# Delta-rule scan on four quarters of the array, differential attention's values product in query halves, and the order planned anew

## The chip, the cores and the metric

The program runs on one core of a Trainium2 chip. The metric is the device time of one execution in microseconds (us); lower is better. Engines: PE multiplies matrices, DVE, ACT and POOL work element by element, SP issues most DMAs; each runs its own instructions in the order in which they stand, and waits where an operand is not there yet.

## What is computed

One layer over 256 tokens of width 1024. The branches share one projection; each has heads of width 64, four of them, and its own gate.

```python
h = rmsnorm(x, pre_norm_g[l])
proj = jnp.einsum('btd,dc->btc', h, w_in[l])          # (256 x 1024) @ (1024 x 4104)
p_gdn, p_hgrn, p_moba, p_diff = jnp.split(proj, splits, axis=-1)
y = jnp.concatenate([gdn_branch(p_gdn, ...), hgrn2_branch(p_hgrn, ...),
                     moba_branch(p_moba, ...), diff_branch(p_diff, ...)], axis=-1)
y = jnp.einsum('btc,cd->btd', y, w_out[l])
x = x + rmsnorm(y, post_norm_g[l])
```

The two places that change are the scan of the gated delta rule (chunks of 64 tokens, so four steps) and the last product of differential attention:

```python
def step(S, inp):
    q_c, k_c, u_c, w_c, a_c, d_c = inp
    v_new = u_c - w_c @ S
    o = q_c @ S + a_c @ v_new
    S = S * d_c[..., None, None] + jnp.einsum('bhcd,bhce->bhde', k_c, v_new)
    return S, o
...
outs.append(jnp.einsum('bhqk,bhkd->bhqd', a1 - lam * a2, v[:, :, :e]))
```

## The kernel before

**How work is recorded and ordered.** The program first records every operation in a `Core` object, and only then issues them, all from one line (L392 in the profile; table loads of ACT from L390). Between the two stands `plan()`, a list scheduler: each operation has a rank, which is its longest path to the end plus a fixed lead for the part of the program to which it belongs (`LEAD`: g the delta rule, h HGRN2, m and M the two parts of MoBA, d and D those of differential attention, o the output projection, x the rest); each engine takes the ready operation of highest rank, except that a change of ACT's function table is put off by up to `HOLD` of rank and a change of PE's tiling mode by up to `STAY`. The sequence that results is fixed in the program.

**Projections.** Weights arrive by DMA as `raw` blocks, which ACT rounds to `whi` and DVE turns into a remainder `wlo`; the activations stand likewise as `hT_hi` and `hT_lo`. Each tile of a projection takes three products (hi by hi, lo by hi, hi by lo) into a bank `pj`. These are most of PE's work, and the filling between all other steps.

**Delta rule.** Before the scan, an inverse of each 64x64 chunk matrix is made: 15 steps of substitution inside 16x16 blocks on DVE (`g_nb`, `g_y`), a transposition by DVE into `g_xa`, products `gA<-g_xa,g_ee` and `gB<-g_ya,g_za`, and the same once more with 32x32 tiles. The scan (lines 804 to 840) then has four steps n. Two heads share the 128 partitions, head hh on partitions 64hh to 64hh+63; two such pairs hp make four products per operation. In step n > 0: `kb` by the state `st` into bank gB, DVE subtracts (`g_r`), and `qd` by `st` into bank gA (`po`, which collects o of all steps). Then the inverse by `g_r` into gB, which ACT copies to `g_vn`; for n < 3 `kd` by `g_vn` into gB and DVE's new state `g_s`; and `aq` by `g_vn` into gA. In the trace `kb` and `qd` both read as g_eb, `kd` as g_kdec and `aq` as g_ee. All of these products use a 64x64 quarter of the array, always the same two: rows 0 to 63 with columns 0 to 63, and rows 64 to 127 with columns 64 to 127. Each is float32 and leaves two records in the trace, so four products are x8.

**Differential attention.** `attend` multiplies transposed probabilities (`d_pt`, 128 keys by 128 queries) by values (`v_diff`, 128 keys by 64), 12 products of full height and width into one bank wB, which leave 24 records. Its logits (`wB<-d_st`) read operands that POOL's queue assembles by 24 DMA copies from `d_ks` and `qk4k`.

**The end.** Output projection (`pj<-whi,y_gdn` and on, into pj and gA), a norm on ACT and DVE, four output DMAs.

Of the kernel before, what the change touches and what calls it, by code (L numbers as in the profile page):

```python
# [29 lines left out]
D = 1024  # L30
# [61 lines left out]


class Op:
    __slots__ = ("eng", "fn", "args", "kw", "cost", "need", "preds", "succs", "rank", "left", "at", "order", "boost", "groups", "work", "part", "lat", "mode")


class Core:
# [2 lines left out]

    SETS = {AF.Exp: 6, AF.Ln: 6, AF.Silu: 18}
    OUT = ("out", "accum_out", "dst")
    HOLD = 34479
    SWITCH, KEEP, STAY = 95, 1e9, 8733
    LEAD = {'h': 7522, 'g': 6523, 'o': -111940, 'M': 5144, 'x': 39478, 'm': 28417, 'd': 3696, 'D': 2624}
    WINDOW = 4096 / 1.2
    LAT = {"PE": 200, "DVE": 170, "ACT": 170, "POOL": 170, "SP": 2600}

    def __init__(self, ctx, tc):  # L110
        self.tc, self.nc = tc, tc.nc
        nc = tc.nc
        self.sb = ctx.enter_context(tc.tile_pool(name="sb", bufs=1))
        self.ps = ctx.enter_context(tc.tile_pool(name="ps", bufs=1, space=bass.MemoryType.PSUM))
        ctx.enter_context(tc.manual_schedule())
        self.engines = {"PE": nc.tensor, "DVE": nc.vector, "ACT": nc.scalar, "POOL": nc.gpsimd, "SP": nc.sync}
        self.ops = []
        self.boost, self.part = 0.0, "x"
        self.phys, self.turn, self.masks = {}, {}, {}
        self.sbuf, self.psum = {}, {}  # L120

# [50 lines left out]
    def record(self, eng, fn, cost, writes, reads, args, kw, need=None):  # L172
        op = Op()
        op.eng, op.fn, op.args, op.kw, op.cost, op.need = eng, fn, args, kw, cost, need
        op.preds, op.succs, op.boost, op.groups, op.work = set(), [], self.boost, (0, 1, 2, 3), 0.0
        op.part, op.lat, op.mode = self.part, self.LAT[eng], (128, 128)
        me = len(self.ops)
        for w, aps in ((False, reads), (True, writes)):
            for ap in aps:
                name = ap.tensor.name  # L180
                if name in self.psum:

                    b = self.psum[name]
                    if b[0] != eng:
                        b[0], b[1], b[2] = eng, b[2], []
                    if me not in b[2]:
                        op.preds.update(b[1])
                        if eng == "PE":

                            start = kw.get("start", True)  # L190
                            op.preds.update(i for i in b[2] if start or self.ops[i].kw.get("start", True))
                        b[2].append(me)
                    continue
                q, m = self.region(ap)
                log = self.sbuf.setdefault(name, [])
                keep = []
                for e in log:
                    i, wi, qi, mi = e
                    hit = (w or wi) and q & qi and m & mi and i != me
                    if hit:  # L200
                        op.preds.add(i)
                    if not (hit and w and qi & ~q == 0 and mi & ~m == 0):
                        keep.append(e)
                keep.append((me, w, q, m))
                self.sbuf[name] = keep
        self.ops.append(op)
# [17 lines left out]
    def mm(self, out, lhsT, rhs, start=True, stop=True, **kw):  # L224
        n, m = self.size(rhs), lhsT.shape[1]
        full = 1.667 if rhs.dtype == F else .417
        cost = max(n * full, m * full) + 2 if rhs.dtype == F else max(n * .446, 107) + 4.5
        self.record("PE", "matmul", cost, [out], [lhsT, rhs], (out,),
                    dict(lhsT=lhsT, rhs=rhs, start=start, stop=stop, **kw))
        p, m = self.rows(out)  # L230
        o = self.ops[-1]
        if 2 < m < 128:
            o.groups = tuple(range(p // 32, (p + m + 31) // 32))
        k = self.rows(rhs)[1]
        o.mode = (32 if k <= 32 else 64 if k <= 64 else 128 if k > 96 else 96, 32 if m <= 32 else 64 if m <= 64 else 128)
        o.work = n * full * k / 128

    def tr(self, out, in_, ident):
# [56 lines left out]
    def plan(self, noise=None):  # L295

        import heapq
        ops = self.ops
# [9 lines left out]
        for i, o in enumerate(ops):  # L308
            o.rank += o.boost + (self.LEAD.get(o.part, 0.0) if o.boost < BOOST else 0.0)
            if noise is not None:  # L310
                o.rank += noise[i]
        ready = {e: [] for e in self.engines}
        free = dict(PE=1150.0, DVE=880.0, ACT=800.0, POOL=0.0, SP=800.0)
        events = [(0.0, 0, i) for i, o in enumerate(ops) if not o.left]
        due = {}
        heapq.heapify(events)
        order, cur = [], 6
        cols, mode, work = [0.0] * 4, (128, 128), {}
        while events:
            t = events[0][0]  # L320
            while events and events[0][0] <= t:
                _, kind, i = heapq.heappop(events)
                if kind == 0:
                    heapq.heappush(ready[ops[i].eng], (-ops[i].rank, i))
            for e, q in ready.items():
                if not q or free[e] > t:
                    continue
                i = heapq.heappop(q)[1]
# [29 lines left out]
                if e == "PE":  # L358

                    if o.mode != mode:  # L360
                        o.at = max(t, max(cols) + self.SWITCH)
                        mode = o.mode
                    else:
                        o.at = max([t] + [cols[g] for g in o.groups])
                    k = int((o.at + 630) / self.WINDOW)
                    slow = 1 if work.get(k - 1, 0.0) >= .41 * self.WINDOW else 2
                    work[k] = work.get(k, 0.0) + o.work
                    end = o.at + cost * slow
                    for g in o.groups:
                        cols[g] = end  # L370
                    free[e] = end if len(o.groups) == 4 else o.at + 7 * slow
                heapq.heappush(events, (free[e], 1, -1))
                for s in o.succs:
                    n = ops[s]
# [31 lines left out]
def _build(c, x, pxt, w_in, w_out, cst, prow, out, dbg):  # L406
# [231 lines left out]
    def gdn(pv, pab, sq):  # L638
# [168 lines left out]
        kd5 = kd.rearrange("p j q hp d -> p (j q) hp d")  # L807
        vb5 = vb.rearrange("p j q hp d -> p (j q) hp d")
        heads = [(hp, hh, slice(64 * hh, 64 * hh + 64)) for hp in range(2) for hh in range(2)]
        pair = lambda p: p[:, 0:128].rearrange("p (a b) -> p a b", a=2)  # L810
        for n in range(4):
            tok = slice(n * 64, (n + 1) * 64)
            rr = vb5[:, n]
            if n:
                pw = c.bank("gB")
                for hp, hh, r in heads:
                    mm(pw[r, hp * 64:(hp + 1) * 64], kb[r, hp, tok], st[r, hp, :])
                rr = c.tmp("g_r", [128, 2, 64])
                c.tt(rr, vb5[:, n], pair(pw), OP.subtract)
                for hp, hh, r in heads:  # L820
                    mm(po[r, (n * 2 + hp) * 64:(n * 2 + hp + 1) * 64], qd[r, hp, tok], st[r, hp, :],
                       start=False, stop=False, skip_group_check=True)
            pw = c.bank("gB")
            for hp, hh, r in heads:
                mm(pw[r, hp * 64:(hp + 1) * 64], ya4[r, hp, n, :], rr[r, hp, :])
            vn = c.tmp("g_vn", [128, 2, 64])
            act(vn, pair(pw), AF.Copy)
            if n < 3:
                pw = c.bank("gB")
                for hp, hh, r in heads:  # L830
                    mm(pw[r, hp * 64:(hp + 1) * 64], kd5[r, n, hp, :], vn[r, hp, :])
                if n == 0:
                    c.copy(st, pair(pw))
                else:
                    for hp in range(2):
                        c.stt(st[:, hp, :], st[:, hp, :], ed[:, hp, n:n + 1], pw[:, hp * 64:(hp + 1) * 64],
                              OP.mult, OP.add)
            for hp, hh, r in heads:
                mm(po[r, (n * 2 + hp) * 64:(n * 2 + hp + 1) * 64], aq[r, hp, n, :], vn[r, hp, :],
                   start=(n == 0 and hp == 0), skip_group_check=True)  # L840

        s8 = c.tile("g_s8", [128, 8])
        head_norm(s8, po.rearrange("p (a b) -> p a b", a=8), c.tmp("t2k", [128, 8, 64]))
# [3 lines left out]
        po5 = po.rearrange("p (j q hp d) -> p j q hp d", j=2, q=2, hp=2)  # L847
        for hh in range(2):
            for q in range(2):
                r = slice(64 * hh, 64 * hh + 64)  # L850
                c.tt(y[64 * q:64 * q + 64].rearrange("p j (hp hh d) -> p j hp hh d", hp=2, hh=2)[:, :, :, hh, :],
                     po5[r, :, q, :, :], bc(s84[r, :, q, :], 64), OP.mult)
        c.tt(y, y, gz["gdn"], OP.mult)
# [144 lines left out]
    def attend(pt, vm, bank):  # L998

        po = c.bank(bank)  # L1000
        for j in range(2):
            for h in range(4):
                hp, hh = h // 2, h % 2
                o = (j * 4 + h) * 64
                for b in range(j + 1):
                    i = hp if j == 0 else 2 + hp * 2 + b
                    mm(po[:, o:o + 64], pt[:, hh, i, :], vm[:, b, h * 64:(h + 1) * 64], start=(b == 0), stop=(b == j))
        return po.rearrange("p (a d) -> p a d", d=64)

    def attend_t(pt, vm, bank):  # L1010
# [249 lines left out]
```

## Time and profile before

| what | us |
|---|---|
| time, median of 3 runs (lowest, highest) | 168.05 (167.80, 168.16) |
| the profiled execution | 168.47 |
| its span, first to last instruction | 166.7 |
| PE busy | 157.4 (94%) |
| DVE busy | 133.0 (80%) |
| ACT busy | 108.3 (65%) |
| POOL busy | 18.8 (11%) |

The profiled execution lies 168.47 - 166.7 = 1.8 us over its span, and 0.42 us over the median. A record of PE runs from issue to a modelled end, and records overlap: x8 of mean 220 ns may fill 0.23 us. The step from start to start is therefore the cost of one, not its duration. The chain of waits gives such steps directly: each row there is the time that a piece adds to the chain.

### The profile page before, as it was taken

To read this page: it belongs to the slowest core of one execution; us is meant where nothing else is said; L and a number is where in the kernel's file an instruction comes from. 1 tells how busy PE (TensorE), PEld (TensorE's weight loads), DVE (VectorE), ACT (ScalarE), POOL (GpSimd) and SP (SyncE) were. 2 spreads that over 40 slices of the span, in tenths; PEclk is the share of its full clock that TensorE was granted. 3 is DMA by queue.
4 is the path that set the end of the run, shared out by engine and by line. 5 is a ranking of instruction groups with operands and counts; after the bars stand their busy time and mean duration, and the time that the engine had idled before them with its cause. 6 is when DMAs were issued, how large, how long until landed. Compare 5 with 4: busy or idle time off the path is not lost.

```text
span 166.7 us, 3622 instructions
## 1 busy us (share of the span) xinstructions
PE 157.4 (94%) x1351; PEld 138.1 (83%) x1351; DVE 133.0 (80%) x356; ACT 108.3 (65%) x214; POOL 18.8 (11%) x39
## 2 busy tenths in 40 slices
PE   7899999999999999997999999999999999999950
PEld 5699999999886989996899968877778798987850
DVE  0779589998999999996898598699699977428472
ACT  3678459999169986550059987999599353650450
POOL 8600000000001000077065200000000000000000
PEclk9999999999999999999999999999999999999998
DMA  5999998177870005936359886148603400000033
GB/s 165 317 413 412 361 397 322 29 241 225 275 261 0 0 4 168 309 91 128 127 153 243 179 264 240 34 145 286 236 0 129 126 0 4 0 0 0 0 126 126
DMA packets 14256, 27.24 MB, mean 163 GB/s; under 512 B 1440, under 2 KB 2720, under 8 KB 14240
## 3 DMA queue, kind: packets, MB, share of 16 engines
q1 hardware_dynamic: 12944, 25.31, 44.8%
q0 software_dynamic: 1152, 1.57, 4.8%
q8 instruction: 10, 0.16, 0.4%
q10 hardware_dynamic: 144, 0.15, 0.3%
q14 instruction: 6, 0.05, 0.1%
HBM read 24.14 MB, written 1.05 MB: 151 GB/s over the span
## 4 chain that ended last, share of the span: by engine, by line
PE 60%; DVE 23%; DMA 9%; issue 3%; ACT 2%; SPq 1%; DVEq 0%; ACTq 0%
PE pj L392 39%; DMA raw<-in_w_in_dram 9%; PE gA L392 7%; PE gB L392 6%; PE wB L392 4%; PE wA L392 4%; DVE g_nb L392 4%; DVE wlo L392 3%; DVE g_ee L392 2%; DVE y L392 1%; DVE g_kdec L392 1%; DVE g_y L392 1%; DVE prob L392 1%; ACT whi L392 1%; DVE g_vb L392 1%
## 5 line engine op out<-in xcount | busy, mean ns | idle before, releaser
L392 DVE TENSOR_TENSOR wlo<-raw,whi 128x1024 fp32r<-128x1024 f32 (+2 forms) x42 | 48.3, 1173 | 12.4 <-ACT whi L392 7.6
L392 ACT ACTIVATE whi<-raw 128x1024 fp32r<-128x1024 f32 (+2 forms) x41 | 41.0, 1023 | 6.8 <-DMA raw<-in_w_in_dram 3.6
L392 PE MATMUL pj<-hT_hi,whi 128*128 128x256 f32 x144 | 36.8, 289 | 0.7 <-ACT hT_hi L392 0.7
L392 PE MATMUL pj<-hT_lo,whi 128*128 128x256 f32 x144 | 36.5, 288 | 0.0
L392 PE MATMUL pj<-hT_hi,wlo 128*128 128x256 f32 x144 | 28.7, 284 | 0.0
L392 PEld LDWEIGHTS pj<-hT_hi,whi 128*128 128x128 f32 x144 | 26.6, 190 | 1.9 <-ACT hT_hi L392 1.4
L392 PEld LDWEIGHTS pj<-hT_lo,whi 128*128 128x128 f32 x144 | 26.3, 188 | 0.3 <-issue 0.2
L392 PE MATMUL pj<-whi,hT_lo 128*128 128x512 f32 (+2 forms) x80 | 26.3, 348 | 0.0
L392 PEld LDWEIGHTS pj<-hT_hi,wlo 128*128 128x128 f32 x144 | 22.0, 189 | 0.4 <-issue 0.2
L392 PE MATMUL pj<-whi,hT_hi 128*128 128x512 f32 (+2 forms) x64 | 21.2, 344 | 0.0
L392 PE MATMUL pj<-wlo,hT_hi 128*128 128x512 f32 (+2 forms) x64 | 19.9, 353 | 0.2 <-DVE wlo L392 0.2
L392 PEld LDWEIGHTS pj<-whi,hT_lo 128*128 128x128 f32 x80 | 15.0, 188 | 1.6
L390 ACT ACT_TABLE_LOAD x11 | 14.1, 1283 | 1.4 <-PEq L1250 1.2
L392 PEld LDWEIGHTS pj<-whi,hT_hi 128*128 128x128 f32 x64 | 12.0, 189 | 1.2
L392 PEld LDWEIGHTS pj<-wlo,hT_hi 128*128 128x128 f32 x64 | 11.1, 189 | 1.6 <-DVE wlo L392 0.4
L392 ACT ACTIVATE prob<-prob,mx 128x128 f32<-128x128 f32 (+1 forms) x24 | 10.6, 445 | 0.1
L392 DVE CUSTOM_DVE_ANT_0 prob<-wB,cs 128x128 f32<-128x128 f32 (+1 forms) x24 | 8.0, 354 | 1.7 <-PE wB L392 1.6
L392 PE MATMUL pj<-whi,d_st 128*128 128x512 f32 (+1 forms) x32 | 9.1, 371 | 0.0
L392 POOL MEMSET vexp<- 128x1024 f32 x3 | 2.8, 948 | 46.6 <-PE wB L392 46.6
L392 POOL DMA_DIRECT2D d_st<-d_ks x12 | 6.2, 514 | 16.8 <-ACT d_ks L392 16.8
L392 ACT ACTIVATE t2k<-pj 128x512 f32<-128x512 f32 (+1 forms) x4 | 2.2, 544 | 8.9 <-PE pj L392 8.9
L392 ACT ACTIVATE g_za<-gA 32x256 f32<-32x256 f32 x2 | 0.8, 376 | 9.9 <-PE gA L392 9.8
(271 smaller groups left out, 301.0 us busy)
## 6 DMA issues: line engine op xcount, KB each, us to landing
raw<-in_w_in_dram SPq DMA_DIRECT2D x26, 512.0 KB, 5.5
raw<-in_w_out_dram SPq DMA_DIRECT2D x8, 512.0 KB, 4.8
raw<-in_w_in_dram SPq DMA_DIRECT2D x4, 520.0 KB, 9.9
raw<-in_w_in_dram SPq DMA_DIRECT2D x4, 256.0 KB, 4.1
xs<-in_x_dram SPq DMA_DIRECT2D x2, 512.0 KB, 8.4
prob<-in_pxt_dram SPq DMA_DIRECT2D x3, 256.0 KB, 6.1
d_st<-d_ks POOLq DMA_DIRECT2D x12, 64.0 KB, 3.1
d_st<-qk4k POOLq DMA_DIRECT2D x12, 64.0 KB, 3.5
```

The source lines that it names most:

```text
L390: nc.scalar.add_instruction(mybir.InstLoadActFuncSet(name=nc.get_next_instruction_name(), act_func_set_id=cur, ins=[], outs=[]))
L392: getattr(self.engines[o.eng], o.fn)(*o.args, **o.kw)
```

## The change

**Scan.** `qd` by `st` and `aq` by `g_vn` (the side products) write `po` on the other half of the partitions (`other[hh]`), so they use the two quarters that were idle: rows 0 to 63 with columns 64 to 127, and the reverse. `both()` records them pair by pair behind the chain products `kb` by `st` and `kd` by `g_vn`, and gives the eight of a group one rank (`tie`), the highest among them. The last step's `aq` (n = 3) has no chain product beside it. The assembly of y reads `po` from the other half. No operation is added.

**attend.** Each 128x128x64 product becomes two of 64 queries, on the left and the right 64 columns of the array: 24 products for 12.

**Planner.** The model of PE holds 16 quarters' ends in place of four column groups, adds 20 ns to a product that does not fill the array, and has other numbers for `HOLD`, `STAY` and all of `LEAD`. The sequences of all engines are thus planned anew. PE's first 309 rows stay the same; behind them they differ everywhere.

```diff
-    HOLD = 34479
-    SWITCH, KEEP, STAY = 95, 1e9, 8733
-    LEAD = {'h': 7522, 'g': 6523, 'o': -111940, 'M': 5144, 'x': 39478, 'm': 28417, 'd': 3696, 'D': 2624}
+    HOLD = 10718
+    SWITCH, KEEP, STAY = 95, 1e9, 10757
+    LEAD = {'h': 2055, 'g': 7404, 'o': -103025, 'M': 12770, 'x': 27161, 'm': 33539, 'd': 8615, 'D': -9392}
...
+        a, b = (range(x // 32, (x + n) // 32) if n < 96 else range(4) for x, n in ((q, o.mode[0]), (p, o.mode[1])))
+        o.groups = tuple(4 * i + j for i in a for j in b)
+        if len(o.groups) < 16:
+            o.cost += 20
...
+        for tied in ties.values():
+            top = max(o.rank for o in tied)
+            for o in tied:
+                o.rank = top
...
+        other = [slice(64, 128), slice(0, 64)]
+        def both(name, chain, side):
+            c.tie = name
+            for hp in range(2):
+                for f in (chain, side):
+                    for a, hh, r in heads[2 * hp:2 * hp + 2]:
+                        f(a, hh, r)
+            c.tie = None
...
-                for hp, hh, r in heads:
-                    mm(pw[r, hp * 64:(hp + 1) * 64], kb[r, hp, tok], st[r, hp, :])
+                both(f"g{n}s", lambda hp, hh, r: mm(pw[r, hp * 64:(hp + 1) * 64], kb[r, hp, tok], st[r, hp, :]),
+                     lambda hp, hh, r: mm(po[other[hh], (n * 2 + hp) * 64:(n * 2 + hp + 1) * 64], qd[r, hp, tok],
+                                          st[r, hp, :], start=False, stop=False, skip_group_check=True))
                 rr = c.tmp("g_r", [128, 2, 64])
                 c.tt(rr, vb5[:, n], pair(pw), OP.subtract)
-                for hp, hh, r in heads:
-                    mm(po[r, (n * 2 + hp) * 64:(n * 2 + hp + 1) * 64], qd[r, hp, tok], st[r, hp, :],
-                       start=False, stop=False, skip_group_check=True)
...
+            pw = c.bank("gB") if n < 3 else None
+            both(f"g{n}v", lambda hp, hh, r: pw is None or mm(pw[r, hp * 64:(hp + 1) * 64], kd5[r, n, hp, :], vn[r, hp, :]),
+                 lambda hp, hh, r: mm(po[other[hh], (n * 2 + hp) * 64:(n * 2 + hp + 1) * 64], aq[r, hp, n, :],
+                                      vn[r, hp, :], start=(n == 0 and hp == 0), skip_group_check=True))
...
-                    mm(po[:, o:o + 64], pt[:, hh, i, :], vm[:, b, h * 64:(h + 1) * 64], start=(b == 0), stop=(b == j))
+                    for u in (slice(0, 64), slice(64, 128)):
+                        mm(po[u, o:o + 64], pt[:, hh, i, u], vm[:, b, h * 64:(h + 1) * 64], start=(b == 0), stop=(b == j))
```

**Where rows moved: PE in the scan, second step.** Before, from the inverse's product to the next projection tile:

```order
L392 MATMUL gB_118<-g_r_141,g_ya 64x64 x4
L392 MATMUL pj_94<-wlo_104,hT_hi 128x512
L392 MATMUL pj_94<-whi_103,hT_lo 128x512
L392 MATMUL gB_118<-g_vn_142,g_kdec 64x64 x4
L392 MATMUL gA_83<-g_vn_142,g_ee 64x64 x4
L392 MATMUL pj_94<-whi_103,hT_hi 128x512
```

Now:

```order
L401 MATMUL gB_118<-g_r_141,g_ya 64x64 x4
L401 MATMUL pj_94<-whi_103,hT_lo 128x512
L401 MATMUL wA_78<-ident,prob_69 128x128 x2
L401 MATMUL gB_118<-g_vn_142,g_kdec 64x64 x2
L401 MATMUL gA_83<-g_vn_142,g_ee 64x64 x2
L401 MATMUL gB_118<-g_vn_142,g_kdec 64x64 x2
L401 MATMUL gA_83<-g_vn_142,g_ee 64x64 x2
L401 MATMUL pj_94<-whi_103,hT_hi 128x512
```

Four chain products and four side products, which stood one behind the other, now alternate in twos. There are six such groups.

**PE at the values product of differential attention.** Before:

```order
L392 MATMUL gA_83<-ident,m_pt 128x128 x4
L392 MATMUL wB_150<-v_diff,d_pt 128x64 x4
L392 MATMUL pj_94<-whi_97,y_gdn 128x512
L392 MATMUL pj_95<-whi_97,y_gdn 128x512
L392 MATMUL pj_109<-whi_97,y_gdn 128x512
L392 MATMUL pj_94<-whi_100,y_gdn 128x512
L392 MATMUL pj_95<-whi_100,y_gdn 128x512
L392 MATMUL gB_118<-vexp_86,h_kd 64x256 x4
L392 MATMUL gA_83<-vexp_87,h_kd 64x192 x4
L392 MATMUL wB_150<-v_diff,d_pt 128x64 x7
L392 MATMUL gB_118<-m_pt,kf 128x128 x4
```

Now:

```order
L401 MATMUL gB_118<-vexp_86,h_kd 64x256 x4
L401 MATMUL gA_83<-vexp_87,h_kd 64x192 x4
L401 MATMUL wB_150<-v_diff,d_pt 64x64 x10
L401 MATMUL pj_110<-wlo_104,hT_hi 128x512
...
L401 MATMUL pj_109<-whi_97,y_gdn 128x512
L401 MATMUL wB_150<-v_diff,d_pt 64x64 x14
L401 MATMUL gB_118<-h_v,ath 128x64 x4
```

The product, before in runs of 1, 4 and 7, stands in runs of 10 and 14 halves; the first of them right behind HGRN2's 64-column products.

**DVE ahead of the inverse's first transposition.** Before, from the third substitution step from the end:

```order
L392 TENSOR_TENSOR g_nb_134<-g_nb_134,g_y_133 128x8x2
L392 TENSOR_TENSOR g_y_133<-g_y_133,g_nb_134 128x8x2
L392 TENSOR_TENSOR g_nb_135<-g_nb_135,g_y_133 128x8
L392 TENSOR_TENSOR g_y_133<-g_y_133,g_nb_135 128x8
L392 TENSOR_TENSOR g_ya<-g_y_133,cs 128x512
L392 STREAM_TRANSPOSE g_xa<-g_ya 128x512
```

Now:

```order
L401 TENSOR_TENSOR wlo_98<-raw_102,whi_97 128x2x512
L401 TENSOR_TENSOR wlo_101<-raw_105,whi_100 128x2x512
L401 TENSOR_TENSOR wlo_104<-raw_111,whi_103 128x2x512
L401 TENSOR_TENSOR wlo_107<-raw_112,whi_106 128x2x512
L401 TENSOR_TENSOR g_nb_135<-g_nb_135,g_y_133 128x8
L401 TENSOR_TENSOR qk4k<-qk4k 128x512
L401 TENSOR_TENSOR g_y_133<-g_y_133,g_nb_135 128x8
L401 TENSOR_TENSOR gz_moba<-pj_95,rrow 128x512
L401 TENSOR_TENSOR g_ya<-g_y_133,cs 128x512
L401 STREAM_TRANSPOSE g_xa<-g_ya 128x512
```

Four `wlo` splits and `gz_moba`, which stood behind `g_xa`, and the last split of `qk4k`, which stood seven substitution steps earlier, now stand close ahead of it. On PE, the products that read `g_xa` moved too: 437 projection products stand ahead of them before, 476 now.

## Rows read from the trace of the kernel before

**Rows 1.** The page: busy time of each engine, share of the span, instructions.

```profile
PE 157.4 (94%) x1351; PEld 138.1 (83%) x1351; DVE 133.0 (80%) x356; ACT 108.3 (65%) x214; POOL 18.8 (11%) x39
```

**Rows 2.** The page: the chain that ended last, shares by engine.

```profile
PE 60%; DVE 23%; DMA 9%; issue 3%; ACT 2%; SPq 1%; DVEq 0%; ACTq 0%
```

**Rows 3.** Windows: stretch, its length, busy time per engine; PE clock, DMA share, GB/s.

```profile
25.00:77.20 52.20, 50.84 (x426) 47.42 (x425) 50.45 (x171) 38.79 (x77) 6.08 (x12) 1.00 0.51 159
77.20:160.80 83.60, 83.54 (x759) 69.59 (x759) 64.13 (x150) 53.65 (x109) 6.71 (x14) 1.00 0.39 116
```

**Rows 4.** Chain of waits, scan's last steps: start, us added, engine, written bank, records.

```profile
112.35 0.38 PE gB L392 x8
112.73 0.23 PE gA L392 x8
112.96 1.14 PE pj L392 x4
...
117.06 0.40 PE gA L392 x8
```

**Rows 5.** Groups by shape on PE: the side products that read g_vn.

```profile
L392 PE MATMUL gA<-g_vn,g_ee 64*64 64x64 f32 x32 | 1.6, 221 | 0.0
```

**Rows 6.** Chain of waits, values product of differential attention.

```profile
128.38 0.84 PE wB L392 x8
...
132.12 1.71 PE wB L392 x14
```

**Rows 7.** Timeline of PE: the first of these products and what follows; start, us.

```profile
122.99 0.33 PE L392 MATMUL wB<-v_diff,d_pt 128*128 128x64 f32 x2
123.14 1.18 PE L392 MATMUL pj<-wlo,hT_hi 128*128 128x512 f32 x4
```

**Rows 8.** Chain of waits, MoBA's values product (wB) and HGRN2's state products (gB, gA).

```profile
110.85 1.50 PE wB L392 x16
...
137.87 0.41 PE gB L392 x19
...
138.45 0.27 PE gA L392 x15
138.71 0.43 PE pj L392
```

**Rows 9.** Timeline of PE: the shapes of those products.

```profile
110.78 1.57 PE L392 MATMUL wB<-m_pt,v_moba 128*64 128x256 f32 x16
...
138.07 0.25 PE L392 MATMUL gA<-sall,m_pt 64*32 64x64 f32 x3
138.11 0.23 PE L392 MATMUL gB<-sall,m_pt 64*32 64x64 f32 x3
```

**Rows 10.** Timeline of PE ahead of the inverse; in brackets idle time, and who ended it.

```profile
74.81 0.29 PE L392 MATMUL pj<-hT_lo,whi 128*128 128x256 f32 x1
74.93 0.28 PE L392 MATMUL pj<-hT_hi,whi 128*128 128x256 f32 x1
...
77.19 1.15 PE L392 MATMUL gA<-g_xa,g_ee 64*64 64x64 f32 x32 [1.03 <-DVE g_xa L392]
...
80.48 0.44 PE L392 MATMUL wB<-d_st 128*128 128x128 f32 x2
```

**Rows 11.** Timeline of DVE: a split, what follows it, and rows up to the transposition.

```profile
65.86 1.22 DVE L392 TENSOR_TENSOR wlo<-raw,whi 128x1024 fp32r<-128x1024 f32 x1
66.99 0.25 DVE L392 TENSOR_TENSOR g_y<-g_y,g_nb 128x88 f32<-128x88 f32 x1
...
73.20 0.69 DVE L392 TENSOR_TENSOR qk4k<-qk4k 128x512 fp32r<-128x512 f32 x1
...
75.70 0.69 DVE L392 TENSOR_TENSOR g_ya<-g_y,cs 128x512 f32<-128x512 f32 x1
76.43 0.71 DVE L392 STREAM_TRANSPOSE g_xa<-g_ya 128x512 f32<-128x512 f32 x1
...
88.53 0.69 DVE L392 TENSOR_TENSOR gz_moba<-pj,rrow 128x512 f32<-128x512 f32 x1
```

**Rows 12.** Timeline of POOL's queue, and the copies' time to landing.

```profile
74.66 0.50 POOL L392 DMA_DIRECT2D d_st<-d_ks  x1
...
DMA to landing us min/median/max: 1.8/3.3/5.8
```

**Rows 13.** Chain of waits: PE's last piece.

```profile
159.74 1.08 PE gA L392 x9
```

More of the change, by code (lines that the diff above doesn't have):

```diff
@@ L94 @@
 class Op:
-    __slots__ = ("eng", "fn", "args", "kw", "cost", "need", "preds", "succs", "rank", "left", "at", "order", "boost", "groups", "work", "part", "lat", "mode")
+    __slots__ = ("eng", "fn", "args", "kw", "cost", "need", "preds", "succs", "rank", "left", "at", "order", "boost", "groups", "work", "part", "lat", "mode", "tie")
 class Core:
@@ L117, in __init__ @@
         self.ops = []
-        self.boost, self.part = 0.0, "x"
+        self.boost, self.part, self.tie = 0.0, "x", None
         self.phys, self.turn, self.masks = {}, {}, {}
@@ L174, in record @@
         op.eng, op.fn, op.args, op.kw, op.cost, op.need = eng, fn, args, kw, cost, need
-        op.preds, op.succs, op.boost, op.groups, op.work = set(), [], self.boost, (0, 1, 2, 3), 0.0
-        op.part, op.lat, op.mode = self.part, self.LAT[eng], (128, 128)
+        op.preds, op.succs, op.boost, op.groups, op.work = set(), [], self.boost, range(16), 0.0
+        op.part, op.lat, op.mode, op.tie = self.part, self.LAT[eng], (128, 128), self.tie
         me = len(self.ops)
@@ L229, in mm @@
                     dict(lhsT=lhsT, rhs=rhs, start=start, stop=stop, **kw))
[L230 to L234, printed above, removed]
+        (p, m), (q, k), o = self.rows(out), self.rows(rhs), self.ops[-1]
         o.mode = (32 if k <= 32 else 64 if k <= 64 else 128 if k > 96 else 96, 32 if m <= 32 else 64 if m <= 64 else 128)
+        a, b = (range(x // 32, (x + n) // 32) if n < 96 else range(4) for x, n in ((q, o.mode[0]), (p, o.mode[1])))
+        o.groups = tuple(4 * i + j for i in a for j in b)
+        if len(o.groups) < 16:
+            o.cost += 20
         o.work = n * full * k / 128
@@ L311, in plan @@
                 o.rank += noise[i]
+        ties = {}
+        for o in ops:
+            if o.tie is not None:
+                ties.setdefault(o.tie, []).append(o)
+        for tied in ties.values():
+            top = max(o.rank for o in tied)
+            for o in tied:
+                o.rank = top
         ready = {e: [] for e in self.engines}
@@ L317, in plan @@
         order, cur = [], 6
-        cols, mode, work = [0.0] * 4, (128, 128), {}
+        cols, mode, work = [0.0] * 16, (128, 128), {}
         while events:
@@ L370, in plan @@
                         cols[g] = end
-                    free[e] = end if len(o.groups) == 4 else o.at + 7 * slow
+                    free[e] = end if len(o.groups) == 16 else o.at + 12 * slow
                 heapq.heappush(events, (free[e], 1, -1))
@@ L827, in gdn @@
             act(vn, pair(pw), AF.Copy)
+            pw = c.bank("gB") if n < 3 else None
+            both(f"g{n}v", lambda hp, hh, r: pw is None or mm(pw[r, hp * 64:(hp + 1) * 64], kd5[r, n, hp, :], vn[r, hp, :]),
+                 lambda hp, hh, r: mm(po[other[hh], (n * 2 + hp) * 64:(n * 2 + hp + 1) * 64], aq[r, hp, n, :],
+                                      vn[r, hp, :], start=(n == 0 and hp == 0), skip_group_check=True))
             if n < 3:
-                pw = c.bank("gB")
-                for hp, hh, r in heads:
-                    mm(pw[r, hp * 64:(hp + 1) * 64], kd5[r, n, hp, :], vn[r, hp, :])
                 if n == 0:
@@ L837, in gdn @@
                               OP.mult, OP.add)
-            for hp, hh, r in heads:
-                mm(po[r, (n * 2 + hp) * 64:(n * 2 + hp + 1) * 64], aq[r, hp, n, :], vn[r, hp, :],
-                   start=(n == 0 and hp == 0), skip_group_check=True)
         s8 = c.tile("g_s8", [128, 8])
@@ L849, in gdn @@
             for q in range(2):
-                r = slice(64 * hh, 64 * hh + 64)
+                r = other[hh]
                 c.tt(y[64 * q:64 * q + 64].rearrange("p j (hp hh d) -> p j hp hh d", hp=2, hh=2)[:, :, :, hh, :],
```

## The prediction, made before the changed kernel ran

> **What bounds the kernel now.** I read the busy times first: PE is busy for 157.4 of 166.7 us [rows 1], and the chain that ended last runs over PE for 60% and over DVE for 23% of the span [rows 2]. An average hides where the two change places, so the windows come next. From 25.00 to 77.20 us PE is idle for 52.20 - 50.84 = 1.36 us and DVE for 52.20 - 50.45 = 1.75; both are nearly full there. From 77.20 to 160.80 PE is idle for 0.06 us by the records, and DVE for 19.5 [rows 3]. PE's clock was granted in full in both stretches (1.00, the 2.4 GHz level), so no time is to be had from it. The timeline shows the one long stop of PE in the middle: 1.03 us at 77.19, for DVE's `g_xa` [rows 10]. So: behind 77 us every step that PE saves moves the end, unless a wait takes its place, and ahead of 77 us DVE decides when the inverse may start. PE's last piece ends at 159.74 + 1.08 = 160.82 [rows 13]; the tail behind it is not touched by the change.
>
> **The scan's side products.** In the chain the chain products of a step add 0.38 us and the side products behind them 0.23 [rows 4]; the 0.15 between the two is the price of coming from another tiling mode. There are six such groups (the 24 records of three `qd` groups, and 24 of the 32 in [rows 5]); the seventh, `aq` of the last step, stays alone at 0.40 [rows 4]. If the four quarters work at once, a group costs 0.38 in place of 0.61: 6 x 0.23 = **-1.38 us**, all on PE behind 77 us. If they don't, 0. Nearest rows: HGRN2's state products use tiles of 64x32 in both halves of the rows, into gB and gA, whose records interleave from 138.07 on [rows 9]; 19 records of 64 columns take 0.41 us and 15 take 0.27, so 18 to 22 ns each [rows 8]. The scan's records, of the same 64 columns in two quarters, take 0.23 / 8 = 29 ns each. More tiles at work thus do give more, across both halves of the rows and into two banks, which is the shape of the changed group. I take the full gain. The tie costs the chain little: the second pair of chain products now stands behind two side products, at most 0.06 us (a quarter of 0.23) each time.
>
> **The values product in halves.** The 24 records take 0.84 + 1.71 us in two runs [rows 6] and 0.15 for the first (122.99 to 123.14) [rows 7], 2.70 in all. That is 0.22 per product of 64 columns, against 0.23 / 4 = 0.058 for a scan product of as many columns, so it isn't the columns that cost here; a weight load of the whole width is what the scan's products lack. Afterwards there are 48 records of 64 columns on half the width. MoBA's values product is the nearest: 128x64 tiles in two column halves, eight records of 256 and eight of 128 columns [rows 9], which is 48 times 64 columns, in 1.50 us [rows 8], or 1.35 without the mode change. There a weight serves two or four times as many columns, though, so its loads are better covered. With scan and MoBA both at 28 to 29 ns per 64 columns I take 48 x 29 ns = 1.39, **-1.31 us**. The other end, halves one behind the other at 58 ns a record: 2.78, no gain (+0.08). Both runs must now change the tiling mode, which before cost nothing there.
>
> **Mode changes.** Over the whole sequence PE changes mode 49 times, before 46. At 0.15 each (0.38 - 0.23, [rows 4]) that is **+0.45 us**.
>
> **The new order ahead of `g_xa`.** Here the change pays. Four splits now stand ahead of `g_xa` on DVE, each 1.13 us from start to start (65.86 to 66.99), and `gz_moba` with 0.69 at most [rows 11]: 4 x 1.13 + 0.69 = 5.2 us. `g_xa` ended at 76.43 + 0.71 = 77.14, so it would end at 82.3; if DVE also recovers all of its 1.75 us of idleness [rows 3], at 80.6. On PE 39 more projection products stand ahead, 0.12 us each (74.81 to 74.93) [rows 10]: PE had got there at 77.19 - 1.03 = 76.16, and now gets there at 80.8. Its wait thus goes from 1.03 to 1.5, with ends of 0 and, if the fill itself waits for one split, 2.6. I take **+0.45 us**. The filling isn't lost: those products no longer have to be done later, and the splits that DVE does early leave it free behind the inverse, where `g_ya` and the logits' steps interleave with them now.
>
> **The copies for the logits.** The last split of `qk4k` ended at 73.20 + 0.69 = 73.89; now it stands behind the four splits, and with `g_ya` and `g_xa` (0.73 + 0.71), `gz_moba` (0.69) and a short step (0.19) behind it, it ends near 82.3 - 2.3 = 80.0 [rows 11]. POOL's copies that read it are issued 0.5 us apart, and land 3.3 us later in the median, 5.8 at most [rows 12]: 83.8. PE wants the first logits, which it took at 80.48, 3.3 us behind the start of the inverse [rows 10], some 9 projection products further on: 82.3 + 1.15 + 9 x 0.12 = 84.5. The cover was 80.48 - (74.66 + 0.50 + 3.3) = 2.0 us and is now 0.7. I put this at nothing; with 5.8 in place of 3.3 it is 1.8 us, and all behind it on PE waits, since its queue is in order.
>
> **Sum.** -1.38 - 1.31 + 0.45 + 0.45 = -1.8 us. The profiled execution took 168.47; 168.47 - 1.8 = 166.7. It lay 0.42 over the median of 168.05, so the forecast for the median is **166.3 us**. Behind the inverse the order is also new (waits for ACT's `g_za`, `g_vn` and the softmax), and I see neither a gain nor a loss larger than 0.7 us there; that goes into the range.
>
> **Rivals.** *A, the quarters don't work at once.* Then both gains vanish and what is left is +0.45 + 0.45 + 0.08: 168.05 + 1.0 = 169.0; with the halves alone failing, 167.7. For it speaks that in the scan and in `attend` two of the tiles share a half of the rows, and that nothing in the kernel runs these very shapes. Against it speak the 18 to 22 ns, where four tiles of 32 columns stand in each half of the rows [rows 8]. The Trainium skill (TensorE: Matmul & The Clock Gate, Part 3, "The mechanism") says that a weight load overlaps running products only when the row group differs, which speaks against both edits: two tiles beside each other would take turns, and the time would be that of this rival. HGRN2's records do not agree with it.
>
> *B, the start of the inverse becomes the bound.* Slower than before: `qk4k` is late on DVE, its copies take the longest landing, and PE stands for 1.8 us at the first logits on top of the 1.5 at `g_xa`; or one split in the filling is late by its whole 1.13 us, and both ends come together. -1.8 + 1.8 + 1.1 = +1.1: 169.1. It decides from 1.8 us of added standstill on, that is, when copies land 0.7 + 1.8 = 2.5 us later than the median. For it: DVE is full up to there, and the cover has shrunk to 0.7. Against it: the maximum is one of 24 copies.
>
> *C, DVE keeps up.* With its idleness recovered `g_xa` is there before PE, the wait of 1.03 goes too, and the splits done early save waits behind the inverse: -1.38 - 1.31 + 0.45 - 1.03 = -3.3: 164.8.
>
> *D, the planner's order spoils about what the quarters gain.* DVE and ACT deliver later at several places behind the inverse, by 0.3 to 0.5 us at each of four: +1.7, so 168.0.
>
> **Chances.** Forecast 0.50 (its own range 165.5 to 167.3), A 0.13 (half of it with the halves alone failing), B 0.14, C 0.13, D 0.10. Leaving out the far half of C and the upper parts of A and B, 164.9 to 168.8 holds 0.8. A measurement of this kernel can tell about 0.2% (0.34 us) from no change. Slower than 168.4: B, half of A, a quarter of D: 0.22. Within: half of D, a little of A and of the forecast's edge: 0.09. Faster: 0.69.
>
> **What would show it.** Right: in the changed trace, six scan groups whose gB and gA records interleave and add 0.38 to 0.42 us together; `wB<-v_diff` with 48 records in about 1.4 us plus a mode change for each of two runs; PE's standstill at `g_xa` near 82 us of 1 to 2 us; the last piece of PE ending near 159. Wrong: groups that still take 0.6 (A); a bracket of a DMA or of POOL's copies ahead of the first `wB<-d_st` (B); no standstill at `g_xa` (C); short brackets behind ACT or DVE all over the scan (D).

## The result: slower by 0.8%, and the profile after

The changed kernel took 170.07 us in the median against 168.51 for the kernel before (20 runs each): a ratio of 1.0078, 95% interval 1.0058 to 1.0099. Ratios here and below are of the mean times, without the few executions that took over 1.5% longer than the fastest of their kernel. The forecast was 166.3, faster; the range ended at 168.8. So the sign was wrong, and the range too short. The profiled execution took 170.51 us, its span 168.8.

The page of the changed kernel, busy times and the shares of the chain that ended last:

```profile
PE 156.3 (93%) x1375; PEld 136.2 (81%) x1375; DVE 132.5 (79%) x356; ACT 108.2 (64%) x214; POOL 19.0 (11%) x39
...
PE 78%; ACT 7%; DVE 6%; DMA 3%; issue 3%; SPq 1%; DVEq 0%; ACTq 0%
```

PE does 1.1 us less by its busy time [rows 1] and yet ends later: its last piece began at 159.74 [rows 13] and now does at 161.79 in the chain of waits, 2.05 us later.

```profile
161.79 1.08 PE gA L401 x9
```

Where it stops is plain in PE's timeline (start, us, engine, line, operation, records; in brackets idle time and what ended it):

```profile
80.75 0.28 PE L401 MATMUL pj<-hT_lo,whi 128*128 128x256 f32 x1
81.93 1.15 PE L401 MATMUL gA<-g_xa,g_ee 64*64 64x64 f32 x32 [0.90 <-DVE g_xa L401]
...
83.95 0.28 PE L401 MATMUL pj<-hT_lo,whi 128*128 128x256 f32 x1
86.56 0.51 PE L401 MATMUL wB<-d_st 128*128 128x128 f32 x2 [2.33 <-issue]
87.01 1.98 PE L401 MATMUL gB<-g_ya,g_za 64*64 64x64 f32 x32
88.91 0.79 PE L401 MATMUL wB<-d_st 128*128 128x256 f32 x2
```

The standstill at `g_xa` is 0.90 us, about what it was (1.03, [rows 10]). A second one of 2.33 us stands ahead of the first logits. No engine is named as its releaser ("issue"); the runs below show that it was the landing of a DMA. Then the next steps are slow themselves: `gB<-g_ya,g_za` takes 1.98 us. The windows tell why (length, busy us and instructions of PE, PEld, DVE, ACT and POOL, granted clock of PE, share of the DMA engines, GB/s):

```profile
83.00:84.00 1.00, 1.00 (x12) 0.99 (x8) 0.87 (x2) 0.00 (x0) 0.00 (x0) 1.00 1.04 397
84.00:85.00 1.00, 0.23 (x2) 0.02 (x1) 0.48 (x1) 0.48 (x1) 0.00 (x0) 1.00 0.99 262
85.00:86.00 1.00, 0.00 (x0) 0.00 (x0) 0.00 (x0) 0.98 (x2) 0.00 (x0) 1.00 0.32 88
86.00:87.00 1.00, 0.44 (x2) 0.35 (x2) 0.00 (x0) 0.99 (x2) 0.00 (x0) 0.86 0.00 0
87.00:88.00 1.00, 1.00 (x19) 1.00 (x20) 0.67 (x5) 0.09 (x1) 0.00 (x0) 0.50 0.00 0
88.00:89.00 1.00, 1.00 (x21) 0.88 (x17) 0.00 (x0) 0.00 (x0) 0.00 (x0) 0.50 0.00 0
89.00:90.00 1.00, 1.00 (x5) 1.00 (x6) 0.95 (x2) 0.00 (x0) 0.00 (x1) 0.50 0.00 0
```

Having stood still, PE was granted half its clock (0.50, the 1.2 GHz level) from about 86.8 to 90.1. And the DMA engines were full (0.99 to 1.04) until 85, then empty. What they moved stands in the queues' timelines, and what released it on DVE. First DVE, then SP's weight loads, then POOL's last two copies with their time to landing:

```profile
74.54 4.62 DVE L401 TENSOR_TENSOR wlo<-raw,whi 128x1024 fp32r<-128x1024 f32 x4
...
79.17 0.68 DVE L401 TENSOR_TENSOR qk4k<-qk4k 128x512 fp32r<-128x512 f32 x1
...
81.17 0.71 DVE L401 STREAM_TRANSPOSE g_xa<-g_ya 128x512 f32<-128x512 f32 x1
```

```profile
75.79 0.54 SPq L401 DMA_DIRECT2D raw<-in_w_in_dram  x1
76.92 0.54 SPq L401 DMA_DIRECT2D raw<-in_w_in_dram  x1
78.06 1.68 SPq L401 DMA_DIRECT2D raw<-in_w_in_dram  x2
```

```profile
80.14 0.98 POOL L401 DMA_DIRECT2D d_st<-qk4k  x2 [2.30 <-DVE g_y L401]
...
DMA to landing us min/median/max: 5.8/6.0/6.1
```

Each split that DVE finishes frees a `raw` buffer, and SP loads the next weight block into it at once: four blocks of 512 KB within 4 us. The two last copies, issued at 80.14 behind the late remainder of `qk4k`, run through the full DMA engines and take 6.1 and 5.8 us to land; PE resumes at 86.56.

The two edits themselves did what was forecast. A group of the scan in the chain of waits (start, us added, engine, bank, records), to be held against 0.38 + 0.23 in [rows 4]:

```profile
110.78 0.20 PE gB L401 x2
110.99 0.01 PE gA L401 x2
111.00 0.04 PE gB L401 x2
...
111.18 0.87 PE pj L401 x3
```

From 110.78 to 111.18 are 0.40 us in place of 0.61; the other five groups take 0.38 to 0.39. And the values product, against 2.70 [rows 6, 7]:

```profile
131.64 0.58 PE wB L401 x20
...
136.26 0.96 PE wB L401 x28
```

48 records in 1.54 us, a mode change included.

### The profile page after: what moved, and what is told of

Its sections match the earlier page's. It is cut to its first block, busy times and chain, and to the rows that moved or that the text cites. A ratio compares the mean times of both kernels' runs of the same rounds, so it can differ in the third digit from the quotient of the medians.

```text
span 168.8 us, 3668 instructions
## 1 busy us (share of the span) xinstructions
PE 156.3 (93%) x1375; PEld 136.2 (81%) x1375; DVE 132.5 (79%) x356; ACT 108.2 (64%) x214; POOL 19.0 (11%) x39
## 3 DMA queue, kind: packets, MB, share of 16 engines
HBM read 24.14 MB, written 1.05 MB: 149 GB/s over the span
## 4 chain that ended last, share of the span: by engine, by line
PE 78%; ACT 7%; DVE 6%; DMA 3%; issue 3%; SPq 1%; DVEq 0%; ACTq 0%
PE pj L401 53%; PE gB L401 8%; PE gA L401 6%; PE wB L401 6%; PE wA L401 5%; DMA raw<-in_w_in_dram 3%; ACT whi L401 3%; DVE wlo L401 2%; DVE y L401 1%; ACT L399 1%; SPq L401 1%; DVE b4k L401 1%; ACT d_pt L401 1%; ACT prob L401 1%; ACT t2k L401 0%
## 5 line engine op out<-in xcount | busy, mean ns | idle before, releaser
L401 PE MATMUL pj<-hT_hi,whi 128*128 128x256 f32 x144 | 37.9, 291 | 1.1 <-ACT hT_hi L401 0.9
L401 PE MATMUL pj<-hT_lo,whi 128*128 128x256 f32 x144 | 37.1, 287 | 0.0
L401 PE MATMUL pj<-hT_hi,wlo 128*128 128x256 f32 x144 | 31.6, 288 | 0.7 <-DVE wlo L401 0.7
L401 PEld LDWEIGHTS pj<-hT_hi,wlo 128*128 128x128 f32 x144 | 23.0, 189 | 1.4 <-DVE wlo L401 1.2
L401 PE MATMUL pj<-wlo,hT_hi 128*128 128x512 f32 (+2 forms) x64 | 19.0, 344 | 0.0
L401 POOL DMA_DIRECT2D d_st<-qk4k x12 | 5.9, 501 | 12.4 <-PE wB L401 10.1
```

Source lines behind the costliest of these rows:

```text
L401: getattr(self.engines[o.eng], o.fn)(*o.args, **o.kw)
```

## Experiments

Theory 1: the edits gain about what was forecast, and the new order loses more, by one place: the remainder of `qk4k` comes late, its copies meet four weight blocks, PE stands still, and its clock falls. Rivals: the quarters gain nothing in time; the loss is spread over many waits of the new order; the fall of the clock is a symptom that costs nothing. In the kernels below the sequence of every engine is that of the changed kernel (or of the kernel before) word for word but for what is named: the plan is made, then single operations are moved in it. Two of them, `before_scan` and `before_both`, are planned again with the old numbers, which also moves a few neighbours of the scan. Ratios are to the kernel before, run on the same chip.

**One instruction moved.** After planning, the remainder of `qk4k` (`late`; `ks` is that of `d_ks`) is put behind the first of the four splits:

```diff
         order, _ = self.plan()
...
+        late, ks = self.lo_of
+        dve = [i for i in order if ops[i].eng == "DVE"]
+        first = dve[dve.index(ks) + 1]
+        order.remove(late)
+        order.insert(order.index(first) + 1, late)
```

> The changed kernel with one instruction moved: DVE makes the remainder of qk4k right behind the first of the four weight splits, not behind the fourth; everything else stands as in the changed kernel. Theory 1 (the late copies stop PE, and the stop lowers the clock): DVE is done with it near 76.4 us in place of 79.9, POOL issues the last two copies by 78.4 and they land by 84 even at 5.7 us each; the standstill of 2.33 us at the first logits and the stretch at half clock go, 2.3 + 1.7 us: about 166.1, ratio to before 0.985 to 0.990. Rival (something else holds PE there, or the copies are slow however early they are issued): standstill stays above 1.5 us, ratio above 1.003.

Measured: 166.54 us, ratio 0.9883 (0.9862 to 0.9904). POOL's queue, PE's timeline and PE's last piece in the chain:

```profile
77.60 1.00 POOL L407 DMA_DIRECT2D d_st<-qk4k  x2
...
81.87 1.15 PE L407 MATMUL gA<-g_xa,g_ee 64*64 64x64 f32 x32 [0.69 <-DVE g_xa L407]
83.99 0.34 PE L407 MATMUL wB<-d_st 128*128 128x128 f32 x2
84.25 1.15 PE L407 MATMUL gB<-g_ya,g_za 64*64 64x64 f32 x32
```

```profile
157.87 1.08 PE gA L407 x9
```

The copies leave 2.5 us earlier. They still take 5.4 and 5.1 us to land, beside the same weight blocks, but now that is early enough: the long standstill is gone, `gB<-g_ya,g_za` takes 1.15 us again, and PE's last piece ends at 158.95, where the prediction had put it (near 159). One DVE instruction of 0.6 us at the wrong place thus was worth 1.95% of the time.

**The wait filled.** The wait stays, but PE multiplies something during it, ahead of the first logits product (`first`):

```diff
+            if i == first:
...
+                for _ in range(18):
+                    nc.tensor.matmul(bank, lhsT=tile_last.kw["lhsT"], rhs=tile_last.kw["rhs"], start=True, stop=True)
```

> The changed kernel with 18 extra products of the projection's shape (0.118 us each, 2.1 us) on PE ahead of the first logits product; their result is overwritten, nothing else is changed. If the standstill itself lowers the clock and that costs 1.7 us on top of the wait: clock 1.00 throughout, 168.4, ratio 1.000. If the clock's fall has another cause or costs nothing: ratio stays at 1.008. If PE was not waiting for a fixed landing time there: the fill adds its 2.1 us, ratio 1.02.

Measured: 168.70 us, ratio 1.0007 (0.9983 to 1.0031). The first logits came at 86.13, 0.43 us earlier than in the changed kernel (the copies took 5.8 and 5.6 us to land in this execution), and at full clock (timeline of PE, windows):

```profile
83.95 2.28 PE L403 MATMUL wB<-hT_lo,whi 128*128 128x256 f32 x18
86.13 0.41 PE L409 MATMUL wB<-d_st 128*128 128x128 f32 x2
```

```profile
87.00:88.00 1.00, 1.00 (x25) 0.93 (x22) 0.58 (x4) 0.00 (x0) 0.00 (x0) 1.00 0.06 16
88.00:89.00 1.00, 1.00 (x11) 1.00 (x10) 1.00 (x4) 0.44 (x1) 0.66 (x2) 1.00 0.00 0
```

Useless work on PE made the kernel faster by 1.0078 - 1.0007 = 0.7%, 1.2 us: this is the price of the clock, on average. The rest to `early_split`, 1.0007 - 0.9883 = 1.2% or 2.1 us, is the price of the wait, where theory 1 had 2.3. The average hides that the clock did not fall in every execution. Of the changed kernel's 20, four had a mean granted clock of 0.990 to 0.992 and took 168.5 to 169.1 us, about as long as the filled kernel (0.988 to 0.997); fifteen had 0.979 to 0.985 and took 169.5 to 170.8. Between the means of the two groups lie 1.5 us, so 1.7 was near the price where the clock does fall. How long PE stood still in each is not known, since only one was profiled.

**The weights held back.** SP waits for the copies before it loads the last two of the four blocks. It does so by a small DMA of 6 KB that reads the first `d_st` tile (`seen`) and stands ahead of the third block (`held[0]`):

```diff
         for i in order:
+            if i == held[0]:
+                nc.sync.dma_start(self.scratch[0:96], seen)
```

> The changed kernel with one small DMA of 6 KB added on SP's queue that reads the first d_st tile and so keeps the last two of the four weight blocks that follow (2 x 512 KB) back until POOL's copies have landed; nothing else moves. Theory 1a (the copies are late because the weight blocks fill the DMA engines): the two copies issued at 80.1 to 81.1 land in about 3 us, standstill at most 0.5 us, clock 1.00: ratio 0.985 to 0.993. Rival 1b (the copies are late by their late issue alone, the weights do not matter): landing still near 6 us, ratio stays at 1.008, or higher by the weights that come later.

Measured: 166.70 us, ratio 0.9884 (0.9865 to 0.9903), the same as with the early split. The copies leave as late as in the changed kernel, but with two weight blocks beside them in place of four:

```profile
80.16 0.98 POOL L416 DMA_DIRECT2D d_st<-qk4k  x2 [2.31 <-DVE g_y L416]
...
DMA to landing us min/median/max: 2.5/2.6/2.8
```

```profile
82.00:83.00 1.00, 1.00 (x32) 0.96 (x32) 0.00 (x0) 0.00 (x0) 0.00 (x0) 1.00 0.19 43
83.00:84.00 1.00, 1.00 (x12) 0.97 (x9) 0.85 (x2) 0.00 (x0) 0.00 (x0) 1.00 0.00 0
```

```profile
84.09 0.34 PE L416 MATMUL wB<-d_st 128*128 128x128 f32 x2
```

The DMA engines run empty before 83, the copies land after 2.8 and 2.5 us, and PE starts the logits without waiting. So the late issue alone did no harm; it needed the weight blocks in the way. The Trainium skill (DMA: Bandwidth & Descriptors, "Queues, rings and completion order") says that a DMA engine serves the queues that have work for it in turn, a packet each; by that a copy would share the engines with the blocks, not wait for whole ones. No row here shows the turns. What the rows show is that 64 KB took 2.5 to 2.8 us to land with two blocks beside it and 5.8 to 6.1 with four, so turns or not, the landing got more than twice as long.

**The edits undone in place.** In the changed kernel's sequence the side products go to the same quarters as the chain products, and each pair of halves is one product (the planner still reckons with the quarters of the changed kernel, so the sequence stays):

```diff
-        other = [slice(64, 128), slice(0, 64)]
+        other = [slice(0, 64), slice(64, 128)]
...
+            if o.whole == "skip":
+                continue
+            if o.whole is not None:
+                nc.tensor.matmul(**o.whole)
+                continue
```

> The changed kernel's sequence on every engine, but the side products of the scan use the same two quarters as the chain products (order of issue unchanged), and each product of the values by query halves is one product of full width. So it prices the two edits alone inside the changed kernel. Theory 1 (the edits gain what was forecast, 1.3 for the scan and 1.2 for the halves): 2.5 us slower than the changed kernel, ratio to before 1.022. Rival (quarters do not work at once, or their gain is hidden): same as the changed kernel, ratio 1.008.

Measured: 171.54 us, ratio 1.0163 (1.0119 to 1.0206). The direction is that of theory 1, the size 0.85%, 1.4 us, smaller than 2.5. But the two times don't differ by the edits alone. The standstill was shorter (2.03 us in the profile, not 2.33), and above all the clock fell less often: of the five executions in the ratio, three had a granted clock of 0.993 to 0.996 (mean 170.6 us) and two 0.984 to 0.985 (172.4). Held against the changed kernel's executions at like clock (168.7 and 170.2), the edits are worth 1.9 and 2.2 us, from few executions. The pair was also run again without the standstill:

> The changed kernel's new sequence with the split moved as in early_split, so without the long standstill, and both edits undone in place as in undone_in_place. What is left of the change is the new sequence alone. If the edits carry the gain within the new sequence: 166.5 + 2.1 = 168.6, ratio to before 1.000 (0.997 to 1.004). If the new sequence itself is what gains, once its standstill is gone: ratio 0.990 to 0.993. If it is worse than the old one by as much as the edits gain: above 1.008.

Measured: 168.81 us, ratio 1.0019 (1.0004 to 1.0034), against 0.9883 with the edits: 1.36%, **2.3 us for the edits**, of 2.69 - 0.45 = 2.2 forecast. PE's last piece:

```profile
160.10 1.08 PE gA L413 x9
```

It ends 2.23 us behind that of `early_split`. Laid side by side by their products, the two timelines of PE are 0.1 us apart ahead of the scan, 1.2 behind it and 2.3 behind the values product. The new sequence alone, without its standstill, is nearly as fast as the old one: 0.2% slower (0.04% to 0.34%), some 0.3 us.

**The same edits in the old sequence.** Each alone and both, in the kernel before, with the planner's old numbers. The scan's edit is that of the change; a values product is planned as one and issued as two halves at its place:

```diff
                     mm(po[:, o:o + 64], pt[:, hh, i, :], vm[:, b, h * 64:(h + 1) * 64], start=(b == 0), stop=(b == j))
+                    c.ops[-1].whole = [dict(out=po[u, o:o + 64], lhsT=pt[:, hh, i, u], rhs=vm[:, b, h * 64:(h + 1) * 64],
+                                            start=(b == 0), stop=(b == j)) for u in (slice(0, 64), slice(64, 128))]
...
+            if o.whole is not None:
+                for half in o.whole:
+                    nc.tensor.matmul(**half)
+                continue
```

> The kernel before with the scan's edit alone (side products on the two idle quarters, tied and alternating with the chain products); the planner's numbers are those of before, and its sequence is the same but for the scan's own rows and two or three neighbours. If the quarters work at once: 6 x 0.23 = 1.4 us less, 167.2, ratio 0.992. If their gain is hidden by waits for DVE and ACT in the scan: ratio 0.998 to 1.002.

> The kernel before with the values product of differential attention in query halves alone, each pair of halves at the place of the whole product; all sequences are those of before. If the halves work at once: 1.2 us less for the products, about 0.3 back for two more mode changes: 167.7, ratio 0.995. If not, or if the gain is hidden: ratio 1.000 to 1.003.

> The kernel before with both edits and the sequence of before. If the new sequence of the changed kernel was needed to win from the edits, this gains less than 0.5 us, ratio above 0.997. If the edits carry all of the gain and the new sequence only cost: 2.3 us less, 166.3, ratio 0.986, as fast as the changed kernel with its split moved (0.988).

Measured: the scan alone 167.98 us, ratio 0.9963 (0.9950 to 0.9977); the halves alone 168.09, 0.9983 (0.9973 to 0.9994); both 167.86, 0.9968 (0.9948 to 0.9987). So both edits gain 0.5 us there, not 2.3: the first expectation of `before_both` nearly holds (it said above 0.997), the second fails. Each edit alone lies between its two expectations: 0.6 us for the scan, 0.3 for the halves.

Where the rest goes can be read from the rows of `before_both`. PE hardly stands still: from 95 to 126 us it is idle for 0.11 us (0.06 in the kernel before). The chain that ended last does leave PE for ACT, from 100.44 us on; but so does that of `early_split`, from 108.11 to 119.0, where the edits are worth 2.3 us, so the chain doesn't name the loss. Three things do cost time.

First, PE changes mode 51 times in the trace, against 46 before and 49 in the changed kernel; five more at 0.15 (0.38 - 0.23, [rows 4]) are 0.75 us. Second, five scan groups interleave as in the changed kernel (the one from 99.28 to 99.72 in the chain adds 0.44 us), but that of the last step doesn't stay together: half of its side products go ahead, and a projection product comes between (chain):

```profile
112.95 0.33 PE gA L405 x4
113.28 0.42 PE pj L405
113.71 0.20 PE gB L405 x2
113.91 0.03 PE gA L405 x2
```

Third, behind the second run of the values product PE now comes too early for HGRN2's `gB<-m_pt,kf` and waits for DVE, which is still at `sall` (timeline of PE):

```profile
131.35 0.98 PE L403 MATMUL wB<-v_diff,d_pt 128*64 128x64 f32 x28
132.54 1.16 PE L405 MATMUL gB<-m_pt,kf 64*128 64x128 f32 x8 [0.21 <-DVE sall L405]
133.72 1.16 PE L405 MATMUL gA<-m_pt,kf 64*128 64x128 f32 x8
```

In the kernel before, the `m_pt,kf` products of gA started among those of gB; now they follow one another. From the start of that run to the projection product behind them are 3.46 us (131.35 to 134.81), against 3.34 before (132.06 to 135.40), so what the run itself gained is lost again. No run took one of the three away alone; how they share the missing 1.8 us stays open.

**One more step.** As `early_split`, with `gz_moba` behind `g_xa` on DVE:

> The changed kernel with the remainder of qk4k behind the first of the four weight splits, as in early_split, and gz_moba (0.60 us on DVE) behind g_xa in place of ahead of it. DVE then has g_xa 0.6 us earlier; PE's standstill there was 0.69 in early_split, so 0.6 us more are gained: 165.9, ratio 0.985. If DVE or ACT are late again behind that, ratio 0.988 as early_split.

Measured: 166.34 us, ratio 0.9873 (0.9859 to 0.9887). The standstill at `g_xa` falls from 0.69 to 0.21 us:

```profile
81.52 1.15 PE L415 MATMUL gA<-g_xa,g_ee 64*64 64x64 f32 x32 [0.21 <-DVE g_xa L415]
```

The time falls by 0.1% only, and the intervals overlap, so 0.6 us expected are not seen; PE's last piece began at 157.50 in place of 157.87. This is the fastest version of the study, 1.3% ahead of the kernel before, but not surely ahead of `early_split`.

The changed kernel was run once more beside `early_undone`:

> The changed kernel itself, on the same chip as early_undone, for comparison: ratio to before 1.006 to 1.010, standstill at the first logits above 1.8 us in its profile, a stretch of some 3 us at half clock behind it. Were the standstill an accident of one profiled run, it would be missing here.

Measured: 170.13 us, ratio 1.0086 (1.0060 to 1.0113). Its profile, of an execution of 171.00 us, has the standstill again, at 2.67 us, with 3.4 us at half clock behind it:

```profile
86.93 0.41 PE L401 MATMUL wB<-d_st 128*128 128x128 f32 x2 [2.67 <-issue]
```

The loss is no accident of one chip, and the standstill none of one profile; that of `undone_in_place` has it too (2.03 us).

## Why the prediction was wrong

**The scan's side products:** right. 0.38 to 0.40 per group, as 0.38 was forecast; about 1.2 us over the scan for 1.38.

**The values product in halves:** right. 1.54 us with a mode change, against 1.39 + 0.15. The rule of the Trainium skill in rival A (TensorE: Matmul & The Clock Gate, Part 3, "The mechanism") would have given no gain here; the trace does not agree with it.

**Rival A:** fell. In one and the same sequence the edits are worth 2.3 us.

**`g_xa`:** right in mechanism, the term too high. `g_xa` was ready at 81.17 + 0.71 = 81.88, forecast 82.3; PE got there at 81.03, forecast 80.8; it waited 0.90, forecast 1.5. Against the 1.03 of before that is -0.13 us where the sum has +0.45.

**The copies for the logits: this step failed.** All of its times were close: the remainder ended at 79.85 (forecast 80.0), PE wanted the logits at 84.2 (84.5). But it took 3.3 us as the time to landing, the median of the 24 copies of the trace before, and put the delay at nothing; the last two took 6.1 and 5.8. The copies before ran beside DMA engines that were half idle (busy share 0.41 to 0.68 from 70 to 80 us). What was not followed is what a moved split sets free: its `raw` buffer, and with it a transfer of 512 KB on SP's queue. The prediction priced the four splits on DVE and on PE and left out the four DMAs that they release, which fill the DMA engines exactly while the copies run. `hold_weights` shows that this was the cause: same late issue, two of the four blocks held back, no loss.

**Rival B** was the right mechanism with chance 0.14, and too cheap. It set 1.8 us for the standstill; it was 2.33 in the profile, 2.1 by the runs. The half clock behind it, 1.2 us by the runs, was in no term at all. The +1.1 of B became +1.3 by the ratio (+1.6 by the medians), and the forecast's -1.8 plus 2.1 and 1.2 is +1.5.

**What was right by luck.** "Every step that PE saves moves the end" was read from the windows of the kernel before. In the old sequence it is not so: 0.5 of 2.3 us arrived, the rest lost, as far as its rows tell, to more mode changes, a group that broke up and a wait for DVE. It came true in the new sequence, which the prediction had not seen as a merit of it. With the failed step mended by one instruction, the sum of -1.8 us nearly stands: 168.60 became 166.54, -2.1. Part of that is luck too: the +0.45 for `g_xa` did not come, while the new sequence as a whole cost some 0.3.

## What to carry to other kernels

When a step that frees a buffer moves, follow the buffer: the next transfer into it starts earlier too, and several at once fill the DMA engines for whoever needs a small copy then. Take a copy's time to landing from a stretch in which the DMA engines are as loaded as they will be, not as the median of the trace. And price a standstill of TensorE by more than its length when it may lower the clock: filling the wait with useless products here gave back 1.2 of the 3.3 us. And test an edit in the order in which it will run: the same two edits were worth 2.3 us in one order and 0.5 in the other.

## What the runs showed of the hardware

In three profiles a standstill of TensorE of 2.03, 2.33 and 2.67 us, on an engine that had been busy, was followed by some 3.4 us at half clock; in the other profiles, with no standstill over 1.05 us in that stretch, the clock stayed at 1.00 there. The same kernel did not lose its clock each time: 4 of its 20 executions had a mean of 0.990 or more, the others 0.985 or less.

A copy of 64 KB took 1.8 to 2.0 us to land with the DMA engines about half busy (the kernel before, 72 to 75 us), 2.5 to 2.8 with two weight blocks of 512 KB beside it, and 5.1 to 6.1 with four (`early_split` and the changed kernel).

Products on the four 64x64 quarters run at once: their records start within 0.02 us of one another, and 16 of them, into two banks, take 0.40 us with the mode change. Whether the second bank is needed for that, no run here shows.
